# Reciprocal square root by logarithm and exponential, earlier input loads and a divided last product in an eight-core decoder step

## The chip, the cores and the metric

The kernel runs on all 8 cores of one Trainium2 chip (trn2). Each core does the same program on its own data. The time of a run is the device time of its slowest core, in microseconds (us). A program on eight cores has a slower state in some runs, in which the cores of one die (four of the eight) show a lower granted clock, that is the share of full speed that the profile records for TensorE; only runs outside that state ("fast") are compared, and where a median over all runs is given, the text says so. "The mean core" below is the mean over the eight cores of one fast profiled run.

## The reference

One step of a one-layer decoder: a mixer made of causal pooling and a gated short convolution, then a squared-ReLU MLP, with three RMS norms. Model width is 1024, MLP width 4096, eight prompts of 2048 tokens plus 16 meta tokens, and 512 sample tokens.

```python
def rmsnorm(x, g):
    y = x * lax.rsqrt(jnp.mean(x * x, axis=-1, keepdims=True) + EPS)
    return y * g

def layer(x, ...):
    hn = rmsnorm(x, norm1_g)
    proj = jnp.einsum('btd,de->bte', hn, w_in)      # u | B | C | h
    ...                                             # pooling mixer, y = B * conv3(C * h)
    x = x + jnp.einsum('bte,ed->btd', mix, w_out)
    hn = rmsnorm(x, norm2_g)
    a = jax.nn.relu(jnp.einsum('btd,df->btf', hn, w1))
    x = x + jnp.einsum('btf,fd->btd', a * a, w2)
    return x, ...
...
y_prompt = rmsnorm(xp, final_g)[:, N_META:]
```

## The kernel before

Each core holds one prompt and 64 sample tokens as 8 groups of 264 columns (features on partitions, tokens on columns); group 0 has 280 until the MLP, with the meta tokens. Groups 0 to 2 share the first reading of the input weights, in 16 blocks; groups 3 to 7 follow one by one through the mixer; then the MLP goes over four pairs of groups, twice, once for each half of its width. The MLP uses products of 2x2 blocks in seven multiplications. Early on the pooling weights are multiplied into the output weights (the "folding", eight matmuls of 512 columns). To copy a finished sum out of PSUM is called an eviction. A list scheduler orders each engine's queue from a table of costs written into the kernel, so a changed constant reorders everything.

All work goes through helpers, and the profile names those lines: L572 is a matmul, L594 a ScalarE activation, L597 a tensor_tensor on VectorE or GpSimd, L602 VectorE's scalar_tensor_tensor (two operations, two inputs, one scalar), L606 VectorE's reciprocal, and L618 a DMA (L615 after the change). "psall" is the PSUM, where the matmuls put their sums, "big" the SBUF, which holds everything else on the core. In the views PE is TensorE, PEld its weight loads, DVE VectorE, ACT ScalarE, POOL GpSimd and SPq the queue that issues most DMA transfers; "h2d" holds the normalised input of the MLP, "w1p" and "w2p" its weights.

The norm, used by all three RMS norms but for small differences:

```python
def rs_from(q, n):
    bank = alloc()
    r = ps(bank, n)
    for i in range(2):
        mm(r, ONEB[:], q[i], i == 0, i == 1)        # sum over partitions
    act(r, r, AF.Sqrt, scale=1.0 / D, bias=EPS)
    recip(r, r)
    return r, bank

def n1_ss(g):
    r, bank = rs_from(SQ_(g), NIN[g])
    for k in range(8):
        stt(HN[g][k], XT[g][k], cn(k), r, ALU.mult, ALU.mult)
    free(bank)
```

The convolution, in SBUF, and the order of the first loads and of the first 48 chunks (a chunk is eight matmuls: one weight block on one group):

```python
def conv(dst, z, m, st):
    act(dst, z[c, 2 * st:2 * st + m], AF.Copy, scale=cn(28 + 8 + c))
    stt(dst, z[c, st:st + m], cn(28 + 4 + c), dst, ALU.mult, ALU.add)
    stt(dst, z[c, 0:m], cn(28 + c), dst, ALU.mult, ALU.add)
# ...
for i in range(16):
    load_win(i, ...)                                # 0.5 MB each
ld["x1"] = load_x(1, [ld[0]], "sp")                 # group 1 after weight block 0
ld["x2"] = load_x(2, [ld[3]], "sp")                 # group 2 after weight block 3
# ...
todo = sorted((max(hn_t[g], w_t(i)), i, g) for i in range(16) for g in range(3))
for t, i, g in todo:
    if g not in seen:                               # first chunk of a group
        seen.add(g)
        if g > 0:
            n1_sq(g)                                # squares
            n1_ss(g)                                # sums, norm, products
    ...                                             # the chunk
```

At the end of the last pair the squares of all four quarters of a block are taken at once, two reciprocals follow, and sixteen scalings of 264 columns:

```python
def final(p):
    for h in range(2):
        ...
        mm(r, ONEF[:], FS[h], True, True, f32=True)
        act(r, r, AF.Sqrt, scale=1.0 / D, bias=EPS)
        recip(FS[h], r)
    for d in range(4):
        for q in range(4):
            stt(X[d][q], X[d][q], cn(16 + d + 4 * (q % 2)), FS[q // 2], ALU.mult, ALU.mult)
        finals.append(dma("sync", dr(yT[p, d]), X[d][:], 128 * 4 * GN * 4, tag="y"))
```

Of the kernel before, what the change touches and what calls it, by code (L numbers as in the profile page):

```python
# [84 lines left out]
class Prog:  # L85
# [87 lines left out]
    def schedule(self):  # L173
# [14 lines left out]
        for op in reversed(ops):  # L188
            full = op.dur + (2.0 + op.bytes / 300e3 if op.dma else 0.0)
            p = 0.0  # L190
            for s in succ[op.id]:
                lat = 0.06 if ops[s].eng == op.eng and not op.dma else LAT[op.eng]
                p = max(p, ops[s].prio + lat)
            p += full
            for s in follow[op.id]:
                p = max(p, ops[s].prio + op.dur)
            op.prio = p
# [17 lines left out]
        def release(i, t, op):  # L215
            nonlocal cnt
            for s in succ[i]:
                lat = 0.06 if ops[s].eng == op.eng and not op.dma else LAT[op.eng]
# [168 lines left out]
def build_nc():  # L387
# [211 lines left out]
    def stt(out, a, s, b, op0, op1):  # L599
# [3 lines left out]
                     [out], ins, cost("vector", out.n, "f"))  # L603

    def recip(out, a):
        return P.add("vector", lambda e: e.reciprocal(out=out.ap, in_=a.ap), [out], [a], cost("vector", out.n, "f"))  # L606
# [10 lines left out]
    def dma_(q, out, in_, nbytes, extra, tag, prev):  # L617
        return P.add(q, lambda e: e.dma_start(out=out.ap, in_=in_.ap), [out], [in_], 0.07 if q == "sync" else 0.95, dma=True,  # L618
# [24 lines left out]
    def load_x(g, extra=(), link=None):  # L643
        return dma("sync", XT[g][:], dr(xg[g - 1]), xb, extra=extra, tag="x%d" % g, link=link)

    ld["x0a"] = dma("sync", XT[0][0:4], dr(x0[:, 0:4]), 128 * 4 * 280 * 4, tag="x0a", link="sp")
    dma("sync", CN[0:40], dr(cst), 20480, tag="cst", link="sp")
# [7 lines left out]
    for i in range(16):  # L655
        load_win(i, {0: ["x0a"]}.get(i) and [ld["x0a"]] or [])
    ld["x1"] = load_x(1, [ld[0]], "sp")
    ld["x2"] = load_x(2, [ld[3]], "sp")
    dma("sync", PWR[:], dr(pwT), 1 << 18, extra=[ld[9]], tag="pw", link="sp")
    dma("gpsimd", WR[:], dr(wout[:, 0:4]), 2 * MB, tag="wr")  # L660
    dma("gpsimd", WOUT[4:6], dr(wout[:, 4:6]), MB, tag="wo")
    ld["wo"] = dma("gpsimd", WOUT[6:8], dr(wout[:, 6:8]), MB, tag="wo")
    ld["x3"] = load_x(3, [ld[15]], "sp")
    ld["x4"] = load_x(4, [ld["wo"]], "sp")

    def load_w1(b, c, extra=()):
        op = dma("gpsimd", W1[c][0:4], dr(w1p[b * 8 + c]), MB, extra=extra, tag="w1_%d_%d" % (b, c))
        tsums(W1[c])
        return op

    def load_w2(b, d):
        op = dma("gpsimd", W2[d][0:4], dr(w2p[b * 4 + d]), 2 * MB, tag="w2_%d_%d" % (b, d))
        tsums(W2[d])
        return op

    def tsums(W):
# [6 lines left out]
    def n1_sq(g, parts=2):  # L683
        for i in range(parts):
            s = slice(i * 8 // parts, (i + 1) * 8 // parts)
            act(SQ_(g)[s], XT[g][s], AF.Square)
        q = SQ_(g)
        tt("vector", q[0:4], q[0:4], q[4:8], ALU.add, "b")
        tt("vector", q[0:2], q[0:2], q[2:4], ALU.add, "b")
# [6 lines left out]
    def rs_from(q, n):  # L696
        bank = alloc()
        r = ps(bank, n)
        for i in range(2):
            mm(r, ONEB[:], q[i], i == 0, i == 1)  # L700
        act(r, r, AF.Sqrt, scale=1.0 / D, bias=EPS)
        recip(r, r)
        return r, bank

    def n1_ss(g):
        r, bank = rs_from(SQ_(g), NIN[g])
# [63 lines left out]
    def h_chunk(g, c):  # L770
# [15 lines left out]
        def conv(dst, z, m, st):  # L786
            act(dst, z[c, 2 * st:2 * st + m], AF.Copy, scale=cn(28 + 8 + c))
            stt(dst, z[c, st:st + m], cn(28 + 4 + c), dst, ALU.mult, ALU.add)
            stt(dst, z[c, 0:m], cn(28 + c), dst, ALU.mult, ALU.add)
# [32 lines left out]
    def n2_ss(g):  # L822
# [6 lines left out]
        if g % 2 == 1:  # L829
# [6 lines left out]
            dma("sync", dr(h2d[p], ("h2d", p)), H2P[0:7], 128 * 7 * 4 * GN * 2, tag="h2s")  # L836
# [4 lines left out]
    def fold():  # L841
# [3 lines left out]
        for c in range(4):  # L845
            for h in range(2):
# [3 lines left out]
                act(WOUT[c, h * 512:h * 512 + 512], r, AF.Copy)  # L850
# [21 lines left out]
    n1_sq(0, 4)  # L872
    n1_ss(0)
    hn_t = (9.6, 17.0, 23.0)
    w_t = lambda i: 8.2 + 1.65 * i + (3.2 if i > 1 else 0) + (3.2 if i > 4 else 0)
# [24 lines left out]
    for c in range(5):  # L900
        load_w1(0, c, [ld["x4"]])
# [13 lines left out]
    for g in range(4, 8):  # L915
# [14 lines left out]
        if g == 6:  # L930
            load_h2(0, 0)
# [8 lines left out]
    load_w2(0, 0)  # L940
# [12 lines left out]
    class Unit:  # L953
        def __init__(self, p, b):
            self.p = p
            self.b = b
            self.M = self.K = self.B = None

        def terms(self, j, dst, start, stop, ks):
            r = ps(dst, GN)  # L960
# [44 lines left out]
        m = property(lambda s: ps(s.M, GN))  # L1005
        k_ = property(lambda s: ps(s.K, GN))
        b_ = property(lambda s: ps(s.B, GN))
# [52 lines left out]
    class U2(Unit):  # L1060
        nk = 8

        def __init__(self, p, b, d):
            Unit.__init__(self, p, b)
            self.d = d
            self.X = X[d]
# [4 lines left out]
        def rhs(self, j, k):  # L1071
            return A2[k][AO[j]]
# [7 lines left out]
        def after2(self):  # L1080
            act(self.X[0], self.k_, AF.Copy)

        def after7(self):
            tt("vector", self.X[3], self.m, self.X[3], ALU.add)
            tt("vector", self.X[3], self.b_, self.X[3], ALU.add)

        def after4(self):
            tt("vector", self.X[2], self.m, self.X[2], ALU.add)

        def after3(self):  # L1090
            tt("vector", self.X[1], self.b_, self.X[1], ALU.add)
            if self.b == 0:
                dma("sync", dr(x1d[self.p, self.d], *[("x1d", self.p, self.d, j) for j in range(4)]), self.X[:], 128 * 4 * GN * 4, tag="xs")
            else:
                act(SQF[:], self.X[:], AF.Square)
                if self.d == 0:
                    tt("vector", FS[:], SQF[0:4:2], SQF[1:4:2], ALU.add)
                else:
                    tt("vector", SQF[0:4:2], SQF[0:4:2], SQF[1:4:2], ALU.add)
                    tt("vector", FS[:], FS[:], SQF[0:4:2], ALU.add)  # L1100

    def final(p):
# [126 lines left out]
```

## Time and profile before

| | before |
|---|---|
| median of the first 4 runs, one of them slow | 719.41 us (718.25 to 790.04) |
| spans of the eight cores in the profiled run | 709.8 to 716.7 us |
| mean granted TensorE clock | 0.952 to 0.957 |
| busy on the slowest core: TensorE, VectorE, ScalarE, GpSimd | 87%, 74%, 39%, 14% |

TensorE is the engine with the most work, but no engine is full. The useful question is where TensorE loses time, stage by stage, and what it waits for there; the prediction below does that. One line that it does not show is the chain of work that ended last, by engine, as shares of the span:

```profile
PE 58%; DVE 29%; DMA 6%; ACT 4%; issue 2%; POOL 0%; SPq 0%; DVEq 0%
```

### The profile page before, as it was taken

To read this page: it belongs to the slowest core of one execution; us is meant where nothing else is said; L and a number is where in the kernel's file an instruction comes from. 1 tells how busy PE (TensorE), PEld (TensorE's weight loads), DVE (VectorE), ACT (ScalarE), POOL (GpSimd) and SP (SyncE) were. 2 spreads that over 40 slices of the span, in tenths; PEclk is the share of its full clock that TensorE was granted. 3 is DMA by queue.
4 is the path that set the end of the run, shared out by engine and by line. 5 is a ranking of instruction groups with operands and counts; after the bars stand their busy time and mean duration, and the time that the engine had idled before them with its cause. 6 is when DMAs were issued, how large, how long until landed. Compare 5 with 4: busy or idle time off the path is not lost.

```text
span 716.7 us, 12912 instructions; the slowest of 8 cores (709.8 to 716.7 us)
## 1 busy us (share of the span) xinstructions
PE 623.1 (87%) x5175; PEld 512.8 (72%) x5176; DVE 528.4 (74%) x1302; ACT 282.9 (39%) x715; POOL 103.2 (14%) x121
## 2 busy tenths in 40 slices
PE   2469998598898958999999999989998998998991
PEld 0248886385665847788888888878887887787770
DVE  3556799869999778955746646968859859858866
ACT  2234632252332325505516417307347237337421
POOL 5554141043250800000000001110000000000000
PEclk9779999999998989999999999999999999999995
DMA  7993195832334797795153249999802801500602
GB/s 151 220 207 97 31 174 139 243 122 70 128 87 141 156 162 130 229 319 183 36 193 122 98 142 196 195 184 193 269 1 70 246 36 57 187 1 31 212 1 121
DMA packets 30395, 100.00 MB, mean 140 GB/s; under 512 B 4608, under 2 KB 13824, under 8 KB 26752
## 3 DMA queue, kind: packets, MB, share of 16 engines
q1 hardware_dynamic: 24144, 76.12, 32.7%
q0 software_dynamic: 6192, 23.07, 20.9%
q8 instruction: 40, 0.66, 0.4%
q14 instruction: 19, 0.16, 0.1%
HBM read 88.13 MB, written 34.11 MB: 171 GB/s over the span
## 4 chain that ended last, share of the span: by engine, by line
PE 58%; DVE 29%; DMA 6%; ACT 4%; issue 2%; POOL 0%; SPq 0%; DVEq 0%
PE psall L572 58%; DVE big L597 12%; DVE big L602 12%; DMA big<-w1p 4%; ACT big L594 3%; DVE psall L606 3%; DVE big L606 2%; DMA h2d<-big 2%; DMA big<-x 1%; DVE psall L597 0%; ACT psall L594 0%; SPq L618 0%; POOL big L618 0%; DVEq L327 0%; POOL big L756 0%
## 5 line engine op out<-in xcount | busy, mean ns | idle before, releaser
L572 PE MATMUL psall<-big 128*128 128x264 bf16 (+1 forms) x5175 | 623.1, 282 | 81.1 <-DVE big L597 35.2
L572 PEld LDWEIGHTS psall<-big 128*128 128x128 bf16 x5176 | 512.8, 100 | 190.6 <-DVE big L602 49.9
L597 DVE TENSOR_TENSOR big<-psall,big 128x264 f32<-128x264 f32 (+3 forms) x420 | 173.7, 425 | 120.7 <-PE psall L572 90.0
L594 ACT ACTIVATE big<-psall 128x264 f32<-128x264 f32 (+2 forms) x396 | 144.6, 389 | 223.9 <-PE psall L572 217.9
L597 DVE TENSOR_TENSOR big<-big 128x264 bf16<-128x264 bf16 (+6 forms) x428 | 167.6, 434 | 49.2 <-ACT big L594 40.8
L594 ACT ACTIVATE big<-big 128x264 bf16<-128x264 f32 (+6 forms) x230 | 125.0, 554 | 150.5 <-DVE big L597 143.0
L602 DVE SCALAR_TENSOR_TENSOR big<-big 128x264 bf16<-128x264 f32 (+3 forms) x264 | 116.9, 477 | 3.5 <-ACT big L594 2.0
L597 POOL TENSOR_TENSOR big<-big 128x528 bf16<-128x528 f32 (+14 forms) x54 | 72.0, 1345 | 44.3 <-ACT big L594 42.8
L602 DVE SCALAR_TENSOR_TENSOR big<-big,psall 128x264 bf16<-128x264 f32 (+1 forms) x128 | 52.6, 483 | 1.7 <-DMA h2d<-big 1.5
L594 ACT ACTIVATE psall<-psall 128x264 f32<-128x264 f32 (+1 forms) x88 | 32.9, 382 | 46.2 <-PE psall L572 33.3
L618 POOL DMA_DIRECT2D big<-w1p x16 | 8.6, 545 | 218.1 <-PE psall L572 196.7
L606 DVE RECIPROCAL psall<-psall 128x264 f32<-128x264 f32 (+1 forms) x16 | 28.9, 1813 | 3.0 <-ACT psall L594 3.0
L597 DVE TENSOR_TENSOR psall<-psall,big 128x264 f32<-128x264 f32 x32 | 13.9, 437 | 4.4 <-PE psall L572 2.7
L606 DVE RECIPROCAL big<-psall 128x264 f32<-128x264 f32 x8 | 14.0, 1780 | 1.7 <-ACT psall L594 1.7
L756 POOL COPY big<-big 128x2 f32<-128x2 f32 (+1 forms) x13 | 6.0, 462 | 60.8 <-DVE big L597 58.7
L618 POOL DMA_DIRECT2D big<-w2p x8 | 4.3, 540 | 51.7 <-PE psall L572 51.6
L618 POOL DMA_DIRECT2D big<-win x16 | 8.6, 594 | 5.3 <-DMA big<-x 5.3
L752 POOL COPY big<-big 128x64 f32<-128x64 f32 x7 | 2.8, 401 | 0.0
L618 POOL DMA_DIRECT2D big<-wout x3 | 1.8, 589 | 0.0
L594 ACT ACT_TABLE_LOAD x1 | 1.3, 1283 | 1.1 <-PEq L388 1.1
L622 DVE MEMSET big<- 128x128 bf16 (+1 forms) x2 | 0.3, 165 | 1.2 <-PEq L388 1.2
L843 DVE TENSOR_SCALAR big<-big 128x128 bf16<-128x128 f32 x4 | 0.9, 273 | 0.0
(4 smaller groups left out, 0.4 us busy)
## 6 DMA issues: line engine op xcount, KB each, us to landing
x1d<-big SPq DMA_DIRECT2D x32, 528.0 KB, 5.0
big<-x1d SPq DMA_DIRECT2D x32, 528.0 KB, 5.0
big<-h2d SPq DMA_DIRECT2D x8, 1848.0 KB, 11.3
yT<-big SPq DMA_DIRECT2D x16, 528.0 KB, 3.0
big<-w1p POOLq DMA_DIRECT2D x16, 512.0 KB, 10.2
big<-w2p POOLq DMA_DIRECT2D x8, 1024.0 KB, 14.9
big<-xg SPq DMA_DIRECT2D x7, 1056.0 KB, 9.0
h2d<-big SPq DMA_DIRECT2D x4, 1848.0 KB, 10.3
```

The source lines that it names most:

```text
L572: return P.add("tensor", lambda e: e.matmul(out=out.ap, lhsT=lhsT.ap, rhs=rhs.ap, start=start, stop=stop, skip_group_check=skip), [out], [ ...
L594: return P.add("scalar", lambda e: e.activation(out=out.ap, in_=in_.ap, func=func, **kw), [out], ins, d)
L597: return P.add(eng, lambda e: e.tensor_tensor(out=out.ap, in0=a.ap, in1=b.ap, op=op), [out], [a, b], cost(eng, out.n, kind))
L602: return P.add("vector", lambda e: e.scalar_tensor_tensor(out=out.ap, in0=a.ap, scalar=sv, in1=b.ap, op0=op0, op1=op1), [out], ins, cost(" ...
L606: return P.add("vector", lambda e: e.reciprocal(out=out.ap, in_=a.ap), [out], [a], cost("vector", out.n, "f"))
L618: return P.add(q, lambda e: e.dma_start(out=out.ap, in_=in_.ap), [out], [in_], 0.07 if q == "sync" else 0.95, dma=True, nbytes=nbytes, ext ...
L622: return P.add(eng, lambda e: e.memset(out.ap, v), [out], [], 0.1)
L752: P.add("gpsimd", lambda e: e.tensor_copy(out=U[g][:, 0:16].ap, in_=U[g - 1][:, 264:280].ap), [U[g][:, 0:16]], [U[g - 1][:, 264:280]], 0.2)
L756: P.add("gpsimd", lambda e: e.tensor_copy(out=Z[g][c, 0:2].ap, in_=Z[g - 1][c, 264:266].ap), [Z[g][c, 0:2]], [Z[g - 1][c, 264:266]], 0.1)
L843: P.add("vector", lambda e, c=c: e.tensor_scalar(out=PWS[c].ap, in0=PWR[c].ap, scalar1=cn(24 + c).ap, scalar2=1.0 / POOL_WIN[c], op0=ALU.m ...
```

## The change

The intent is to take VectorE and the loads out of TensorE's way in every stage at once:

1. The reciprocal square root is ln, then exp(-0.5 ln), both on ScalarE, in place of a square root on ScalarE and a reciprocal on VectorE.
2. Groups 1 and 2 are loaded right behind weight block 0; groups 1 to 4 are loaded from GpSimd's queue and the first MLP weights no longer wait for group 4. The squares of groups 0 to 2 come in quarters, and eight matmuls sum them in place of VectorE additions.
3. The convolution builds its sum in a PSUM bank; half of the folding evictions go to VectorE.
4. The last pair's second MLP product is cut into 168 and 96 columns, so that only 96 columns' norm and scaling remain after the last matmul, shared by GpSimd. In every pair the final norm's squares are now taken quarter by quarter, as each comes.
5. Scheduling constants, and two loads held until a store has landed.

```diff
-    def recip(out, a): ...
 # (cut; the next line is the scheduler's cost of a scalar_tensor_tensor)
+                     ..., cost("vector", out.n, "f") + (0.057 if isinstance(s, V) else 0.0))
 # (cut)
+    load_win(0, [ld["cst"]])
+    load_x(1)
+    load_x(2)
+    for i in range(1, 16):
+        load_win(i)
 # (cut)
-    def rs_from(q, n):
+    def rs_from(q, n, nq=2):
 # (cut)
-        act(r, r, AF.Sqrt, scale=1.0 / D, bias=EPS)
-        recip(r, r)
+        act(r, r, AF.Ln, scale=1.0 / D, bias=EPS)
+        act(r, r, AF.Exp, scale=-0.5)
 # (cut)
-        r, bank = rs_from(SQ_(g), NIN[g])
+        r, bank = rs_from(SQ_(g), NIN[g], 8 if g < 3 else 2)
 # (cut)
-            act(dst, z[c, 2 * st:2 * st + m], AF.Copy, scale=cn(28 + 8 + c))
-            stt(dst, z[c, st:st + m], cn(28 + 4 + c), dst, ALU.mult, ALU.add)
-            stt(dst, z[c, 0:m], cn(28 + c), dst, ALU.mult, ALU.add)
+            pb = alloc()
+            t = ps(pb, m)
+            act(t, z[c, 2 * st:2 * st + m], AF.Copy, scale=cn(28 + 8 + c))
+            stt(t, z[c, st:st + m], cn(28 + 4 + c), t, ALU.mult, ALU.add)
+            stt(dst, z[c, 0:m], cn(28 + c), t, ALU.mult, ALU.add)
+            free(pb)
 # (cut)
-    hn_t = (9.6, 17.0, 23.0)
-    w_t = lambda i: 8.2 + 1.65 * i + (3.2 if i > 1 else 0) + (3.2 if i > 4 else 0)
+    hn_t = (11.0, 16.5, 20.0)
+    w_t = lambda i: 10.5 + 1.7 * i + (7.0 if i else 0)
 # (cut)
-            load_h2(0, 0)
+            load_h2(0, 0, [ld["h2s", 2]])
 # (cut)
-    load_w2(0, 0)
+    load_w2(0, 0, [ld["h2s", 2]])
 # (cut)
+            last = b == 1 and p == NP - 1
+            for lo, n in (((0, GN - TN), (GN - TN, TN)) if last else ((0, GN),)):   # TN = 96
+                for t in range(2):
+                    groups.append([U2(p, b, 2 * t, lo, n, lo > 0), U2(p, b, 2 * t + 1, lo, n, lo > 0)])
 # (cut)
-    final(NP - 1)
+    final(NP - 1, GN - TN, TN, True)
```

## The prediction

> **What bounds the kernel now.** I read the list of cores first: spans 709.8 to 716.7 us, clocks 0.952 to 0.957, so no die is disturbed and core 2 can stand for all. TensorE is busy 87% of the span, so I asked not for the busy share but for what TensorE loses in each stage. I cut the span at the first matmul after the first three token groups' input projection (88), at the start of the unbroken MLP (306.5) and at the last MLP matmul (697.2). The view of stretches gives:
>
> ```profile
> core 2: us, PE busy (x) PEld busy (x) DVE busy (x) ACT busy (x) POOL busy (x), PEclk, DMA share, GB/s
> 0.00:88.00 88.00, 58.36 (x394) 40.81 (x396) 49.83 (x92) 33.72 (x71) 38.83 (x54) 0.88 0.70 144
> 88.00:306.50 218.50, 183.49 (x1448) 145.46 (x1445) 191.48 (x423) 81.44 (x197) 57.98 (x55) 0.93 0.60 148
> 306.50:697.20 390.70, 379.11 (x3332) 325.36 (x3332) 273.83 (x767) 165.20 (x445) 6.35 (x12) 1.00 0.48 135
> 697.20:716.70 19.50, 2.15 (x5) 1.18 (x4) 13.26 (x23) 2.54 (x4) 0.00 (x0) 0.61 0.27 111
> ```
>
> In the stretch from 323 to 403 TensorE never pauses: 713 matmuls in 80.0 us, 112.2 ns each. At that rate the first stage is worth 394 x 0.1122 = 44.2 us and loses 43.8; the second is worth 162.5 and loses 56.0; the MLP is worth 373.9 and loses 16.8; the end of 19.5 us is all loss. So 136 us of 717 can be attacked, and the change touches every stage.
>
> The timeline shows what the first stage loses: TensorE ends group 0's chunks at 22.8 and gets nothing to do until group 1 is normalised.
>
> ```profile
> 22.77 0.69 ACT L594 ACTIVATE big<-psall 128x280 f32<-128x280 f32 x2 [0.72 <-PE psall L572]
> ...
> 23.34 2.06 ACT L594 ACTIVATE big<-big 128x1056 bf16<-128x1056 f32 x2
> ...
> 25.43 4.54 DVE L597 TENSOR_TENSOR big<-big 128x1056 bf16<-128x1056 bf16 x2 [8.30 <-ACT big L594]
> ...
> 31.09 1.82 DVE L606 RECIPROCAL psall<-psall 128x264 f32<-128x264 f32 x1 [1.12 <-ACT psall L594]
> 32.94 3.29 DVE L602 SCALAR_TENSOR_TENSOR big<-big,psall 128x264 bf16<-128x264 f32 x8
> ...
> 33.48 10.89 PE L572 MATMUL psall<-big 128*128 128x264 bf16 x64 [2.84 <-DVE big L602]
> ```
>
> The squares of group 1 run at 23.3, behind group 0's evictions, two additions on VectorE take 4.5 us, the reciprocal 1.8, and the product with the norm feeds TensorE one matmul per 0.4 us. Group 2 repeats it (matmuls from 50.6).
>
> In the second stage VectorE is busy 191 of 218 us. Three rows of groups, the first from the page, the others from the view of groups by form in the first 306.5 us (count, busy us, mean ns of one, idle before):
>
> ```profile
> L606 DVE RECIPROCAL psall<-psall 128x264 f32<-128x264 f32 (+1 forms) x16 | 28.9, 1813 | 3.0 <-ACT psall L594 3.0
> ...
> L602 DVE SCALAR_TENSOR_TENSOR big<-big,psall 128x264 bf16<-128x264 f32 x120 | 49.2, 482 | 1.6 <-DMA h2d<-big 1.5
> ...
> L602 DVE SCALAR_TENSOR_TENSOR big<-big 128x264 f32<-128x264 f32 x56 | 31.8, 582 | 2.4 <-ACT big L594 2.0
> ```
>
> A reciprocal costs as much as four other VectorE operations of its size, and the convolution's products, both inputs in SBUF, cost 100 ns more than those with one input in PSUM. The end, from the timeline:
>
> ```profile
> 696.82 1.08 ACT L594 ACTIVATE big<-big 128x1056 f32<-128x1056 f32 x1 [4.58 <-DVE big L597]
> ...
> 703.74 1.81 DVE L606 RECIPROCAL big<-psall 128x264 f32<-128x264 f32 x1 [1.75 <-ACT psall L594]
> ...
> 707.71 6.05 DVE L602 SCALAR_TENSOR_TENSOR big<-big 128x264 f32<-128x264 f32 x15
> 708.94 5.18 SPq L618 DMA_DIRECT2D yT<-big  x4
> ```
>
> Nothing overlaps here: squares and sums until 702, two reciprocals, sixteen scalings until 713.8, then the last store.
>
> **What the Trainium skill says.** "ScalarE: Activation LUTs", section "Table sets: the hidden batching unit", puts exponential and logarithm into one set, with the cheap functions in every set. Then the new pair needs one table load. The trace has one load of 1.28 us for today's functions; it can't show the new set. "SBUF — State Buffer", section "SBUF: two separate sides", says that VectorE operations with two SBUF inputs and GpSimd lock each other out of a shared port pair. The trace agrees: the convolution's 200-column products took up to 1.57 us beside GpSimd and 0.37 without it, by single records. "TensorE: Matmul & The Clock Gate", section "Back-to-back issue gap", gives about 81 ns per matmul with weight load at 128 columns, more than its 56 of pure streaming. No matmul here is that narrow; a weight load lasts 99 ns in the groups' row and hides behind 112. Its Part 1 says that an idle TensorE falls to half clock and recovers after some 3.4 us: the granted share is 0.71 and 0.78 in the stretches 18 to 36 and 36 to 54.
>
> **The change, part by part.**
>
> *Start.* Groups 1 and 2 are loaded right after the first weight block, the squares are cut in four and summed by eight matmuls in place of two large additions, and the norm is two ScalarE passes. By 58.8 us the old kernel had read 17.2 MB (inputs, input and output weights, three groups), landing times from the trace: 303 GB/s, an estimate that I reuse. Constants, group 0 and block 0 are 1.7 MB, group 1 another 1.1: it lands near 12, group 2 near 15 to 16, then one 0.5 MB block per 1.7 us, block 15 near 41. Norm of group 1: four squares of 0.66, a few matmuls, two passes of 0.38, then 3.3 us of products: ready from about 17 to 20; group 2 to 24. TensorE needs 24 x 0.1122 = 2.7 us per block, more than the 1.7 of its arrival, so from about 22 it is its own bound: 48 chunks less the 4 or 5 done, 43 x 0.9 = 39, some half clock, the eight folding matmuls: 394 matmuls done near 67 where 88 stood. Saved 21.
>
> *Second stage.* 13 reciprocals of 1.81 lie in it and 9 of them stand in the chain (its view in order of time has them at 89, 102, 117, 159, 164, 196, 219, 224 and 282); each gives way to one pass of 0.38 plus a handover of about 0.1: 9 x 1.33 = 12 us. The 56 convolution products go from 582 to some 480 ns, 5.7 us of VectorE time, and the 8 short ones some 2; I take half of that as standing in TensorE's way (the view of waits gives it 32 us of waiting in this stage, nearly all on VectorE), so 3 to 4 and I count 2. Folding evictions shared by VectorE: nothing. Against it each convolution takes a PSUM bank for about two microseconds. Saved 14, before that.
>
> *MLP.* At each of three passages to a new token pair in the second half TensorE waits 1.9, 0.85 and 0.4 us while VectorE does reciprocals and scalings (waits put down to the reciprocal: 5.4 us). Without them two thirds go: 6 saved. Cutting the last pair's second product into 168 and 96 columns turns 224 matmuls into 448. By streaming alone this costs nothing; with 81 ns for each of both widths 224 x (162 - 112.2) = 11.2 us; with a full weight load of 98 each, 18.8. I take 5, nearer the streaming side, since the weight loads start as soon as the matmul before has started. Net saved 1.
>
> *End.* Only 96 columns remain: last addition, square, a matmul of sums, two passes and a copy, about 0.25 each with handovers 2 us; ten products on VectorE of 0.25 beside six on GpSimd, 2.6; the store 2.9 as now (713.8 to 716.7). That is 7.5 to 8 in place of 19.5. Saved 11.5.
>
> Sum 21 + 14 + 1 + 11.5 = 47.5, or 672. I take 4 back for PSUM banks and for the reordering of all engines' queues that the new cost constants bring: 676.
>
> **The rivals.** *The narrow matmuls are bound by their weight loads.* For: 99 ns per load, and the skill's 81. Against: the loads' spacing is never tested here. It makes the end of the MLP 6 to 14 us longer: 682 to 690. *The early gain is given back.* The second stage has its own chain: the store of the first residual activations runs from 125.1 to 138.5 and the next norm waits for it, and w1 blocks share the DMA. If that stage is bound by such transfers, removing reciprocals gains 4 and not 14, and part of the 21 waits for weights: 690 to 695. *Two function sets.* If the logarithm and the exponential, or either and the others, alternate between tables, 24 norms pay twice 1.28 us, and more with the drain; about 10 of them stand on the path: 25 us and more lost, 700 or above. The skill speaks against it. *Better than the sum:* TensorE's half-clock stretches in the second stage (0.93 on average, up to 15 us by that alone) close as well: 660.
>
> **Range and chances.** The middle is 676; the first rival alone or half the second gives 685 to 690, the last 660. Both rivals together give 695. So 658 to 695. For less than 2% gain (705) both rivals and more must come true, or the tables: 6%.
>
> **What would show it.** Right: 394 matmuls done by about 67 us; no reciprocals, one table load; convolution products with a PSUM input near 480 ns; no wait over 1 us at passages between pairs; under 9 us from last MLP matmul to the end. Wrong: the spacing of the 96-column matmuls near 100 ns; more than one table load; waits of TensorE on convolutions' banks; the first MLP product not earlier by 25 us than before.

## The result, and the profile after

The kernel after took 675.25 us (median of 11 runs, 674.3 to 722.39, slow ones included); the kernel before took 719.44 us over its 16 runs in those rounds. The ratio of after to before is 0.938, with a 95% interval of 0.9356 to 0.9405: faster by 6.2%. Every ratio here is the mean time of one kernel's fast runs over that of the other's of the same rounds, so not quite the ratio of the medians quoted. The output is correct.

The view of stretches of the slowest core after (core 7), cut at the marks of the prediction. Its columns are those shown there: start:end, length, then busy time and count of TensorE, its weight loads, VectorE, ScalarE and GpSimd, then the granted clock, the DMA share and GB/s. Eighteen matmuls of sums were added in the start, so 394 old matmuls are 412 here:

```profile
0.00:75.20 75.20, 59.49 (x413) 41.91 (x414) 38.14 (x85) 33.23 (x73) 39.71 (x59) 0.98 0.82 168
75.20:279.90 204.70, 172.84 (x1450) 141.73 (x1448) 172.37 (x410) 84.17 (x209) 57.54 (x55) 0.97 0.64 157
279.90:664.70 384.80, 381.28 (x3560) 330.64 (x3558) 274.32 (x847) 184.75 (x528) 6.33 (x12) 1.00 0.47 139
664.70:673.90 9.20, 1.81 (x17) 1.50 (x14) 5.18 (x23) 1.65 (x7) 2.10 (x6) 0.70 0.63 177
```

| stage, slowest core | before | after | saved | predicted |
|---|---|---|---|---|
| start | 88.0 | 75.2 | 12.8 | 21 |
| second stage | 218.5 | 204.7 | 13.8 | 14 |
| MLP | 390.7 | 384.8 | 5.9 | 1 |
| end | 19.5 | 9.2 | 10.3 | 11.5 |
| taken back | | | | -4 |
| sum | 716.7 | 673.9 | 42.8 | 43.5 |

So the total is right, the start was promised 8 too much and the MLP 5 too little. The granted clock of the first two stages rose from 0.88 and 0.93 to 0.98 and 0.97. In the first 27 us this record does not follow the matmuls: it says 1.00 from 24 to 27 us, where those of 264 columns start 0.22 us apart until 26.6 and 0.11 apart after that. And the chain that ended last has changed its make-up:

```profile
PE 59%; DVE 20%; DMA 15%; ACT 3%; issue 1%; POOL 0%; SPq 0%; DVEq 0%
```

VectorE lost nine points of the span, DMA gained nine: transfers now stand where VectorE stood.

**The start.** The timeline view (start, length, engine, line, operation, count, and in brackets how long the engine had been idle and for whom) answers to the lines of before at 22.8 to 33.5:

```profile
19.51 7.94 PE L572 MATMUL psall<-big 128*128 128x264 bf16 x32 [1.40 <-DVE big L602]
...
27.48 0.78 ACT L594 ACTIVATE psall<-psall 128x264 f32<-128x264 f32 x2 [0.44 <-PE psall L572]
28.30 3.29 DVE L602 SCALAR_TENSOR_TENSOR big<-big,psall 128x264 bf16<-128x264 f32 x8 [6.05 <-ACT psall L594]
28.84 20.48 PE L572 MATMUL psall<-big 128*128 128x264 bf16 x152 [1.40 <-DVE big L602]
```

The squares of group 2, four of 0.56 us from 18.84 on in the same view, end at 21.1. Its two norm passes, 0.39 us each, start only at 27.5, when TensorE has done 32 more matmuls in 7.94 us (0.25 us each, twice the full-speed spacing): 24 of chunks, and then the eight sums. VectorE idled 6.05 us for it. After 28.8 TensorE runs without a break for 20 us.

**The second stage.** The view of TensorE's waits gives who was waited for, total, count and the longest. Before (88 to 306.5 us):

```profile
PE psall L572 <- DVE big L602: 19.8, 10, 7.5
```

After (75.2 to 279.9 us):

```profile
PE psall L572 <- DMA big<-h2d: 8.8, 1, 8.8
PE psall L572 <- DVE big L602: 8.7, 4, 3.3
```

The wait for VectorE's products with the norm fell from 19.8 to 8.7 us, its longest, of 7.5 us, is gone, and a DMA wait of 8.8 us has come in: the load of the normalised activations of the first pair ("h2d"), in front of the MLP. Two lines of the timeline show the load's issue and the matmul that it held up:

```profile
217.78 0.33 SPq L615 DMA_DIRECT2D big<-h2d  x1
...
234.06 2.36 PE L572 MATMUL psall<-big 128*128 128x264 bf16 x10 [8.75 <-DMA big<-h2d]
```

**The end.** From the timeline after the last MLP matmul at 664.7, answering to the lines of before at 696.8 to 708.9:

```profile
666.02 0.50 ACT L594 ACTIVATE psall<-psall 128x96 f32<-128x96 f32 x2 [0.22 <-PE psall L572]
667.56 2.10 POOL L597 TENSOR_TENSOR big<-big 128x96 f32<-128x96 f32 x6 [211.75 <-DVE big L1146]
667.56 2.33 DVE L602 SCALAR_TENSOR_TENSOR big<-big,psall 128x96 f32<-128x96 f32 x10
```

Norm and scalings are done at 669.9; before they ended 16.6 us behind the last matmul (713.8 less 697.2), here 5.2.

### The profile page after: what moved, and what is told of

The parts are those of the page before. It is cut to its first block, busy times and chain, and to the rows that moved or that the text cites. A ratio compares the mean times of both kernels' runs of the same rounds, so it can differ in the third digit from the quotient of the medians.

```text
span 673.9 us, 13606 instructions; the slowest of 8 cores (665.7 to 673.9 us)
## 1 busy us (share of the span) xinstructions
PE 615.4 (91%) x5430; PEld 515.8 (77%) x5430; DVE 490.0 (73%) x1361; ACT 303.8 (45%) x816; POOL 105.7 (16%) x132
## 4 chain that ended last, share of the span: by engine, by line
PE 59%; DVE 20%; DMA 15%; ACT 3%; issue 1%; POOL 0%; SPq 0%; DVEq 0%
PE psall L572 59%; DVE big L597 11%; DVE big L602 7%; DMA h2d<-big 4%; DMA big<-w2p 4%; DMA big<-w1p 3%; DMA big<-h2d 2%; ACT big L594 2%; DMA big<-x 1%; ACT psall L594 1%; DMA big<-x1d 1%; DVE psall L602 1%; DVE big L849 0%; DVE psall L597 0%; POOL big L597 0%
## 5 line engine op out<-in xcount | busy, mean ns | idle before, releaser
L572 PE MATMUL psall<-big 128*128 128x264 bf16 (+4 forms) x5430 | 615.4, 275 | 51.2 <-DVE big L602 14.8
L572 PEld LDWEIGHTS psall<-big 128*128 128x128 bf16 (+1 forms) x5430 | 515.8, 99 | 150.7 <-DVE big L602 29.8
L597 DVE TENSOR_TENSOR big<-psall,big 128x264 f32<-128x264 f32 (+5 forms) x440 | 175.2, 411 | 113.0 <-PE psall L572 68.3
L594 ACT ACTIVATE big<-psall 128x264 f32<-128x264 f32 (+3 forms) x404 | 147.1, 384 | 210.6 <-PE psall L572 202.6
L597 DVE TENSOR_TENSOR big<-big 128x264 bf16<-128x264 bf16 (+8 forms) x461 | 173.0, 412 | 41.6 <-ACT big L594 21.6
L597 POOL TENSOR_TENSOR big<-big 128x528 bf16<-128x528 f32 (+15 forms) x60 | 75.4, 1271 | 253.8 <-DVE big L1146 211.7
L602 DVE SCALAR_TENSOR_TENSOR big<-big,psall 128x264 bf16<-128x264 f32 (+4 forms) x174 | 70.7, 466 | 12.9 <-ACT psall L594 12.5
L602 DVE SCALAR_TENSOR_TENSOR big<-big 128x264 bf16<-128x264 f32 (+2 forms) x192 | 76.8, 436 | 1.1
L594 ACT ACTIVATE psall<-psall 128x264 f32<-128x264 f32 (+3 forms) x108 | 39.1, 374 | 27.6 <-PE psall L572 25.5
L594 ACT ACTIVATE psall<-big 128x264 f32<-128x264 f32 (+2 forms) x36 | 16.2, 458 | 29.6 <-DVE big L597 29.3
L602 DVE SCALAR_TENSOR_TENSOR psall<-big,psall 128x264 f32<-128x264 f32 (+2 forms) x36 | 16.3, 459 | 1.3 <-ACT psall L594 1.3
L849 DVE TENSOR_SCALAR big<-big 128x128 bf16<-128x128 f32 x4 | 4.2, 1061 | 0.0
## 6 DMA issues: line engine op xcount, KB each, us to landing
big<-xg POOLq DMA_DIRECT2D x4, 1056.0 KB, 27.5
```

Source lines behind the costliest of these rows:

```text
L572: return P.add("tensor", lambda e: e.matmul(out=out.ap, lhsT=lhsT.ap, rhs=rhs.ap, start=start, stop=stop, skip_group_check=skip), [out], [ ...
L594: return P.add("scalar", lambda e: e.activation(out=out.ap, in_=in_.ap, func=func, **kw), [out], ins, d)
L597: return P.add(eng, lambda e: e.tensor_tensor(out=out.ap, in0=a.ap, in1=b.ap, op=op), [out], [a, b], cost(eng, out.n, kind))
L602: return P.add("vector", lambda e: e.scalar_tensor_tensor(out=out.ap, in0=a.ap, scalar=sv, in1=b.ap, op0=op0, op1=op1), [out], ins, cost(" ...
L849: P.add("vector", lambda e, c=c: e.tensor_scalar(out=PWS[c].ap, in0=PWR[c].ap, scalar1=cn(24 + c).ap, scalar2=1.0 / POOL_WIN[c], op0=ALU.m ...
```

## The experiments

The theory was that each part acts where the prediction put it: the norm pair in all stages, the early loads in the start, the PSUM convolution a little, the split at the end. The rivals: that the narrow matmuls pay for their weight loads, that a transfer takes the place of a removed wait, and that new constants in the scheduler, not the parts themselves, move the time.

To compare stages over kernels with different matmul counts, I used marks on every core and took the mean core: the start lasts to the first 512-column folding matmul, the second stage to the same MLP matmul counted back from the last (3331 before it; 3559 with the split, which adds 224 matmuls and puts four fp32 sums in front of the last), the MLP to the last matmul's start. They lie a few microseconds from the prediction's marks.

| mean core, us | start | second | MLP | end | span | slowest core |
|---|---|---|---|---|---|---|
| before | 83.1 | 222.0 | 389.7 | 19.8 | 714.7 | 716.7 |
| after | 70.5 | 205.9 | 383.8 | 9.3 | 669.5 | 673.9 |
| e1, norm pair alone | 80.3 | 207.8 | 381.5 | 16.7 | 686.3 | 689.7 |
| e3, old loads | 75.5 | 206.1 | 383.6 | 9.3 | 674.5 | 679.5 |
| e8, group 2's sums first | 65.2 | 206.7 | 383.9 | 9.3 | 665.2 | 669.5 |
| e5, convolution in SBUF | 73.2 | 211.3 | 383.7 | 9.3 | 677.5 | 683.6 |
| c, old constants | 68.9 | 209.6 | 383.8 | 9.0 | 671.2 | 677.3 |
| e2, no split | 70.8 | 205.4 | 380.3 | 13.5 | 670.0 | 674.9 |
| e16, e8 and shared scalings | 65.1 | 206.5 | 385.5 | 9.0 | 666.0 | 669.3 |
| e4, free load | 70.6 | 204.9 | 381.8 | 9.3 | 666.6 | 673.9 |
| e10, load in seven parts | 70.6 | 209.1 | 382.5 | 9.3 | 671.5 | 676.5 |
| e12, weights behind the load | 70.3 | 206.6 | 383.8 | 9.3 | 670.0 | 674.3 |
| e14, e8 and e12 | 65.1 | 207.1 | 384.4 | 9.3 | 665.9 | 670.0 |
| e15, e14 with the load free | 65.1 | 208.0 | 381.7 | 9.3 | 664.1 | 670.2 |

The table is of one profiled run each, and small differences in it say little: over its eleven fast runs the mean core of the kernel after has a span of 667.2 to 669.8 us (668.5 on the mean), the profiled one being near the top.

All twelve gave correct results. Edits are against the kernel after, unless said.

### e1: the norm pair alone, in the kernel before

```diff
-        act(r, r, AF.Sqrt, scale=1.0 / D, bias=EPS)
-        recip(r, r)
+        act(r, r, AF.Ln, scale=1.0 / D, bias=EPS)
+        act(r, r, AF.Exp, scale=-0.5)
 # and in final():
-            act(r, r, AF.Sqrt, scale=1.0 / D, bias=EPS)
-            recip(FS[h], r)
+            act(r, r, AF.Ln, scale=1.0 / D, bias=EPS)
+            act(FS[h], r, AF.Exp, scale=-0.5)
```

> The kernel before, with only the reciprocal replaced by the logarithm and exponential pair. If the reciprocals on VectorE held the chain as the prediction counted (12 us in the second stage, about 4 in the start, 5 at the passages between pairs, 3 at the end), the time falls by 20 to 26 us, to about 696. If the chain only named them and other VectorE work or the DMA stores take their place, the gain is under 10 us.

Measured: fast runs 689.23 to 691.23 us, ratio 0.9579 (0.955 to 0.9609). The mean core saves 28.4 us: 2.9 in the start, 14.2 in the second stage, 8.2 in the MLP, 3.1 at the end. The groups of its trace hold one table load, of 1.28 us, as before.

So this one part is about two thirds of the whole gain of 44 us, the two functions share a table, and the rival of two table sets is dead. Of the wait in front of the MLP something more is to be seen in the timeline:

```profile
243.98 3.29 DVE L602 SCALAR_TENSOR_TENSOR big<-big,psall 128x264 bf16<-128x264 f32 x8 [2.09 <-DMA h2d<-big]
...
247.32 5.02 PE L572 MATMUL psall<-big 128*128 128x264 bf16 x22 [8.03 <-DVE big L602]
```

TensorE waits 8.03 us for VectorE, but VectorE itself had waited for a store of activations ("h2d<-big") before it could overwrite its buffer: issued at 225.3, the store landed at 243.95. The name in the view of waits is the last link only; behind it stands the transfer, here already.

### e3: the old order of loads

```diff
-    load_win(0, [ld["cst"]])
-    load_x(1)
-    load_x(2)
-    for i in range(1, 16):
-        load_win(i)
+    for i in range(16):
+        load_win(i, {0: ["x0a"]}.get(i) and [ld["x0a"]] or [])
+    ld["x1"] = load_x(1, [ld[0]], "sp")
+    ld["x2"] = load_x(2, [ld[3]], "sp")
 # (cut: the other loads, hn_t and w_t as before)
```

> The changed kernel with the old order of loads and the old order constants of the first stage; sums by matmuls and the new norm stay. If the early arrival of groups 1 and 2 is what the first stage gained, its 394 old matmuls end near 86 us in place of 75 and the time rises by 9 to 12 us. If the gain came from the sums on TensorE and the shorter norm, the time rises by less than 4.

Measured: 681.12 us, ratio 0.9448 (0.9419 to 0.9478). The start is 5.0 us longer on the mean core, the other stages agree within 0.2. The early loads, with the order constants that belong to them, are worth 5.0 us, between the 9 to 12 and the "less than 4" that were expected; nothing of it is given back later: that rival is wrong for these loads.

### e8: the sums of group 2 ahead of the next weight block

The timeline after suggested that group 2's eight matmuls of sums stand in TensorE's queue behind the chunks of the next weight blocks. The edit asks for squares and sums of group 2 before weight block 1:

```diff
     for t, i, g in todo:
         e = EO[i]
+        if i == 1 and 2 not in seen:
+            seen.add(2)
+            n1_sq(2)
+            n1_ss(2)
```

> The changed kernel with group 2's squares and sums put ahead of the chunks of the second weight block in TensorE's order. In the changed kernel group 2's products start at 28.3 us though its squares are done at 21.1. If that order is the failed part of my start estimate, they start near 25 and the first stage ends 2 to 3 us earlier. Rival: the clock's half rate and block arrivals bound it, and the stage ends within 1 us of 70.5 (mean of the cores).

Measured: 670.2 us (668.72 to 670.99, four fast runs); no run of the kernel after was below 674.3. The ratio to before is 0.9283 (0.9206 to 0.9359, wide since the runs of before were disturbed). The timeline:

```profile
19.51 12.66 PE L572 MATMUL psall<-big 128*128 128x264 bf16 x68 [1.40 <-DVE big L602]
...
24.51 0.79 ACT L594 ACTIVATE psall<-psall 128x264 f32<-128x264 f32 x2 [1.09 <-PE psall L572]
25.33 3.29 DVE L602 SCALAR_TENSOR_TENSOR big<-big,psall 128x264 bf16<-128x264 f32 x8 [3.08 <-ACT psall L594]
```

The products of group 2 start at 25.33 and not at 28.30, and the start is 5.3 us shorter (65.2 against 70.5). That is more than the 2 to 3 expected, and more than the 3.0 by which group 2 starts earlier: in the kernel after TensorE also waits for VectorE for 2.0 us at 51.2, and in this trace it never waits between 19.51 and the end of the stage. So some 3.0 us are the place of eight small matmuls in an in-order queue, and some 2.0 a later wait that went with it, which the expectation did not count. This is the best version: it beats both kernels, by 5 us the one after.

### e5: the convolution in SBUF again

```diff
-            pb = alloc()
-            t = ps(pb, m)
-            act(t, z[c, 2 * st:2 * st + m], AF.Copy, scale=cn(28 + 8 + c))
-            stt(t, z[c, st:st + m], cn(28 + 4 + c), t, ALU.mult, ALU.add)
-            stt(dst, z[c, 0:m], cn(28 + c), t, ALU.mult, ALU.add)
-            free(pb)
+            act(dst, z[c, 2 * st:2 * st + m], AF.Copy, scale=cn(28 + 8 + c))
+            stt(dst, z[c, st:st + m], cn(28 + 4 + c), dst, ALU.mult, ALU.add)
+            stt(dst, z[c, 0:m], cn(28 + c), dst, ALU.mult, ALU.add)
```

> The changed kernel with the convolution's partial results in SBUF again, as before. By the prediction PSUM is worth 2 to 4 us in the second stage (56 products at 582 instead of 480 ns): the time rises by 2 to 4 us and the products with two SBUF inputs come back over 550 ns. Rival: the shorter products hide, or the freed PSUM banks pay them back, and the time stays within 1.5 us.

Measured: 681.98 us, ratio 0.9463 (0.9396 to 0.9531). The mean core loses 8.0 us: 5.4 in the second stage, 2.7 in the start. The view of groups by form (count, busy us, mean ns of one, idle before), first the kernel after:

```profile
L602 DVE SCALAR_TENSOR_TENSOR psall<-big,psall 128x264 f32<-128x264 f32 x28 | 13.7, 489 | 1.3 <-ACT psall L594 1.3
L602 DVE SCALAR_TENSOR_TENSOR big<-big,psall 128x264 f32<-128x264 f32 x28 | 13.4, 483 | 0.4
```

and this experiment:

```profile
L602 DVE SCALAR_TENSOR_TENSOR big<-big 128x264 f32<-128x264 f32 x56 | 37.3, 681 | 3.5 <-ACT big L594 3.1
```

With two SBUF inputs the product takes 681 ns, more than the 582 of the kernel before; with one in PSUM 486. The 56 products cost 37.3 us and 27.1 (13.7 + 13.4), and the time rises by 7 us where 2 to 4 were expected. These means mix two kinds, which the single records part by whether an operation of GpSimd runs at the same time. Alone, 34 of the 56 products take 488 ns, no more than with one input in PSUM; beside GpSimd 22 take 979, up to 2271. With one input in PSUM they take 482 to 490 either way. That agrees with the lock between VectorE and GpSimd that the Trainium skill states ("SBUF — State Buffer", section "SBUF: two separate sides"). In the kernel before 38 lay alone (479 ns) and 18 beside GpSimd (800): in this order more of them meet GpSimd, and each is held longer.

### c_consts: the old scheduling constants

```diff
-                lat = 0.09 if ops[s].eng == op.eng and not op.dma else LAT[op.eng]
+                lat = 0.06 if ops[s].eng == op.eng and not op.dma else LAT[op.eng]
 # (twice)
-                     ..., cost("vector", out.n, "f") + (0.057 if isinstance(s, V) else 0.0))
+                     ..., cost("vector", out.n, "f"))
-        ... 0.07 if q == "sync" else 0.7, ...
+        ... 0.07 if q == "sync" else 0.95, ...
```

> The changed kernel with the scheduler's cost constants as before (0.06 for a handover on one engine, no 0.057 for a per-partition scalar, 0.95 for an issue). The constants change only the order of the engines' queues. I counted them as noise of about 4 us together with PSUM banks: the time should stay within 4 us of 675. If the order is worth more than the parts, it rises by over 4.

Measured: 677.93 us, ratio 0.9397 (0.9334 to 0.946), against 0.938 of the kernel after. The start is 1.6 us shorter and the second stage 3.7 longer. The intervals overlap; by the medians, and by the mean core over all fast runs (671.6 against 668.5), the constants are worth about three microseconds, and do not make the gain.

### e2: no division of the last product

```diff
-            last = b == 1 and p == NP - 1
+            last = False
 # (cut: the end's order of products as in the other groups)
-    final(NP - 1, GN - TN, TN, True)
+    final(NP - 1)
```

> The changed kernel without the cut of the last pair into 168 and 96 columns. By my theory the cut costs under 1 us of TensorE (its matmuls run at 72 and 42 ns in the changed kernel's trace) and takes 4 to 6 us off the end, so this kernel is 4 to 6 us slower than the changed one, near 680. If the narrow matmuls had a hidden cost (11 us by the estimate of 81 ns each), this kernel would be faster than the changed one.

Measured: fast runs 676.44 to 678.38 us, ratio 0.9403 (0.9374 to 0.9432). Undivided, the end is 13.5 us and not 9.3, but the MLP 380.3 and not 383.8. So of the 4.2 us that the split takes off the end it puts 3.5 on the MLP. The whole spans differ by 0.5 us in the two profiled runs (670.0 and 669.5 on the mean core) and by 2.7 over all fast runs (671.2 and 668.5); the medians of the fast runs are 678.05 and 675.25. The intervals of the ratios overlap: the split is worth some 0.5 to 3 us, not the 4 to 6 that were expected. In the kernel after, two stretches of 6.0 and 2.8 us show the divided products at work, the first at 168 and the second at 96 columns:

```profile
643.00:649.00 6.00, 6.00 (x86) 6.00 (x84) 4.90 (x19) 2.07 (x7) 0.00 (x0) 1.00 0.01 3
659.20:662.00 2.80, 2.80 (x71) 2.80 (x68) 2.80 (x16) 2.44 (x10) 0.00 (x0) 1.00 0.03 9
```

The counts include a few matmuls that were still in flight when the stretch began. Read from record to record over all 221 pairs of each width, the median distance from start to start is 73 ns at 168 columns and 43 at 96, against 113 at 264. The weight loads of the same time:

```profile
L572 PEld LDWEIGHTS psall<-big 128*128 128x128 bf16 x73 | 3.2, 98 | 0.0
```

Each load's record lasts 98 ns, but 73 of them lie in a stretch of 3 us: they overlap each other. So 73 + 43 = 116 against 113 ns, times 224, is 0.7 us for the whole division. The first rival, a floor of 81 ns or of a full load, is wrong. From the first 168-column matmul to the start of the last one of 96 columns core 7 needs 29.4 us; the same products undivided, with the 16 other matmuls that lie between, need 26.9 in e2. Of these 2.5 us, 0.7 are the streaming, 0.6 are four fp32 sums of the first part (142 to 212 ns each), which now lie inside the stretch, and 1.2 are four pauses, the longest of 0.55 us behind VectorE in the timeline. The other 1.0 or so lies earlier in the MLP and was not traced.

### e16: e8, and half of the first part's scalings on ScalarE and GpSimd

```diff
 # (on top of e8)
-                if not tail:
+                if not tail and n < GN and d >= 2:
+                    act(x, x, AF.Copy, scale=fg)
+                    tt("gpsimd", x, x, FS[q // 2, lo:hi], ALU.mult)
+                elif not tail:
                     stt(x, x, fg, FS[q // 2, lo:hi], ALU.mult, ALU.mult)
```

> Group 2's sums first, and half of the first part's final scalings (eight of sixteen, 168 columns) moved from VectorE to ScalarE and GpSimd. In the changed kernel six of these sixteen stand in VectorE's queue after the last MLP matmul (1.8 us), and VectorE is busy 7.8 of the 8.7 us before. If VectorE's queue is what the cut of the last pair costs, the end (9.3 us) falls to 7 to 8 and the time by 1 to 3 us below the 670 of the run with the sums first. Rival: ScalarE or GpSimd[...] ends later than VectorE did, and nothing is gained.

Measured: fast runs 670.08 to 673.11 us, ratio 0.9326 (0.9274 to 0.9379); no better than e8. The timeline of it shows why:

```profile
652.30 1.88 DVE L602 SCALAR_TENSOR_TENSOR big<-big 128x168 f32<-128x168 f32 x3
```

GpSimd has eight products of the same shape from 652.26 to 656.7. Three of VectorE's scalings take 1.88 us beside them; three of the same shape took 0.99 us in the kernel after, with GpSimd idle. By single records the four that lie beside GpSimd take 634 ns on the mean and the other four 382. VectorE has eight scalings fewer, but pays for the others. Both operands lie in SBUF, so it looks like e5's loss again. The pauses of the divided product remain.

### e4: the activations' load not held for the store

The wait of 8.8 us in front of the MLP could come from the new condition that the load of the first pair's activations waits for the store of the third pair's. The condition is an order of transfers only; without it the kernel is still correct.

```diff
-            load_h2(0, 0, [ld["h2s", 2]])
+            load_h2(0, 0)
```

> The changed kernel without the added rule that the first load of the MLP input waits for the third pair's store. My theory: this rule made a new wait, 8.8 us of TensorE at 234 us in the changed kernel; without it the load starts some 10 us earlier and the time falls by 5 to 8 us, to about 668. Rival: load and store share the same DMA engines, the wait moves to the store or to the next norm, and the time stays within 2 us of 675.

Measured: 676.11 us, ratio 0.9376 (0.9345 to 0.9408): the same as after. The mean core gains 2.9 us (1.5 over all fast runs), the slowest none: its span is 673.9 as before the edit. The second stage spreads over 198.9 to 211.8 us by core (after: 202.9 to 209.0). On the unlucky core 6 the chain in order of time has a store of activations of 15.3 us (from 207.8) and then this weight load:

```profile
228.29 20.68 DMA big<-w2p
```

It lands at 249, and a wait of TensorE of 8.3 us ends at 251. On core 2 the same two took 12.72 and 13.36 us, and no wait there was over 2.9 us. So the condition costs the early cores something and makes the cores more alike; on the late ones it is not the cause, since a wait as long stands there without it, now for weights.

### e10: the same load in seven parts

If only the first blocks of the load are needed by the first product, seven small loads should let TensorE begin earlier.

```diff
-            load_h2(0, 0, [ld["h2s", 2]])
+            for j in (0, 3, 4, 1, 5, 6, 2):
+                dma("sync", H2[0][j], dr(h2d[0, :, j], ("h2d", 0)), ..., extra=[ld["h2s", 2]], tag="h2l")
```

> The changed kernel with the first load of the MLP input cut into seven loads, one per factor, in the order of use; the rule that they wait for the third pair's store stays. The first product needs one factor in seven. If TensorE's wait of 7 to 10 us at about 230 us is for bytes that it does not need yet, it falls to under 2 us on every core and the time by 5 to 8 us, to about 668. Rival: later factors or the weights hold the next products up just as long, and the gain is under 2.

Measured: fast runs 678.03 to 687.05 us, ratio 0.9441 (0.9325 to 0.9558); not better. In the view of waits, two waits for the load (7.1 and 4.9 us) take the place of the one of 8.8. The timeline of the slowest core:

```profile
226.98 1.07 PE L572 MATMUL psall<-big 128*128 128x264 bf16 x8 [0.53 <-DVE big L602]
...
228.74 1.06 PE L572 MATMUL psall<-big 128*128 128x264 bf16 x8 [0.68 <-DVE big L597]
...
236.89 1.92 PE L572 MATMUL psall<-big 128*128 128x264 bf16 x8 [7.10 <-DMA big<-h2d]
...
243.67 6.53 PE L572 MATMUL psall<-big 128*128 128x264 bf16 x42 [4.86 <-DMA big<-h2d]
```

By the records the first two parts were issued at 220.7 and 221.1, landed at 226.2 and 228.6, and were used at once. The third, of 264 KB, was issued at 221.5 and landed at 236.8: 15.2 us, nearly as long as the whole load of 1848 KB in one piece in the kernel after (217.8 to 233.9, 16.1 us). So the size of the part that TensorE waits for does not set the wait. What the DMA engines have to do beside it may: in the kernel after their busy share is 1.0 from 208 to 232 us.

### e12: the weights of the second product behind the load

```diff
-            load_h2(0, 0, [ld["h2s", 2]])
+            ld["h2l"] = load_h2(0, 0, [ld["h2s", 2]])
-    load_w2(0, 0, [ld["h2s", 2]])
+    load_w2(0, 0, [ld["h2l"]])
```

> The changed kernel with the first two w2 loads waiting for the first load of the MLP input instead of for the third pair's store. In the changed kernel the w2 loads take 43 to 63% of the DMA engines' time between 224 and 232 us, while TensorE waits for the MLP input until 234. If sharing the DMA engines makes that wait, it falls from 7 to 10 us to 3 to 5 and the second stage by 4 to 5 us, the time to about 671. Rival: HBM or the other core of a pair bounds the load, and the gain is under 1.5 us, or the later w2 loads hold up the MLP by as much.

Measured: the median of all six runs is 686.69 us, but three of them were slow; the fast ones are 675.86, 677.79 and 677.89, ratio 0.9405 (0.9377 to 0.9433). The longest wait of the slowest core is 8.8 us, as in the kernel after. That these weights follow so closely does not cause it.

### e14 and e15: e8 joined with e12, and with the load free

```diff
 # e14: the edits of e8 and of e12
 # e15: as e14, but
+            ld["h2l"] = load_h2(0, 0)
```

> Group 2's sums first (5 us alone in its run) and the w2 loads after the MLP input together. If the two are independent the time is 675 less 5 less the gain of the w2 change, about 666; if the earlier start only makes the DMA waits longer, it stays at 670.

> As the combination, and the first load of the MLP input no longer waits for the third pair's store. Freed alone it helped some cores by 8 us and left the slowest where they were. If it was the w2 loads that kept those back, all cores gain now, and the time falls to 660 to 664; if the store and the load slow each other, the slowest core stays within 2 us of the combination's.

Measured: e14 fast runs 670.63 to 671.5 us, ratio 0.9319 (0.9296 to 0.9343); e15 670.87 us, ratio 0.9311 (0.9279 to 0.9342). Both repeat e8's start of 65.1 us, so that gain is confirmed three times (with e16), and neither adds to it. In e15 the mean core is 1.1 us better than in e8 and the slowest 0.7 worse, as in e4.

## Why the prediction was right, and where its steps were not

The total (676 against 675.25) was right. Four terms were mis-sized: the start by -8.2, the end by -1.2, the MLP by +4.9, and the 4 us taken back were not lost. That these cancel to less than one is luck. Of the five signs of being right three came; the 394 matmuls were done at 75.2 and not by 67, and the end took 9.2 and not under 9. One reading of the lines was wrong in its figures: the 200-column products took 1.84 and 1.04 us beside GpSimd and 0.35 to 0.43 without it by the records, not 1.57 and 0.37.

**The start: 21 predicted, 12.8 measured.** The step that failed is "so from about 22 it is its own bound". The prediction expected 4 or 5 chunks done by then; 4 were done (32 matmuls, besides 24 of sums) when, only at 28.8, TensorE came to be fed without a break: 6.8 us late. The prediction gave a norm's sums "a few matmuls" without asking where they stand in TensorE's queue: squares done at 21.1, norm passes at 27.5. e8 moves them and group 2 starts 3.0 earlier. A part was also that the two groups landed at 15.0 and 18.0 us, where "near 12" and "15 to 16" stood. A second piece: the four folding scalings on VectorE, by the groups' rows, take 1061 ns each after and took 273 before (three of the four lie beside GpSimd now, at 1324 ns on the mean, the one alone takes 273); TensorE waits 2.0 us at 51.2 behind them, a wait that is gone in e8. Of the 12.7 us on the mean core, e3 gives 5.0 to the loads, e1 2.9 to the norm pair and e5 2.7 to the convolution in PSUM, and c says that the new constants cost 1.6. The other 3.7 (quartered squares, sums on TensorE) were not measured by themselves; as the parts were added to one kernel or taken from another, they need not add up.

**The second stage: 14 predicted, 13.8 measured.** The sum fits, its parts less so. The norm pair by itself gave 14.2 where 12 were predicted. The convolution was given 2, and undoing it costs 5.4 here and 2.7 in the start; the step "I take half of that as standing in TensorE's way" was too low, and it compared with 582 ns where the alternative in the new order was 681, taking for a fixed cost of two SBUF inputs what only the products beside GpSimd pay. The parts do not add up to the whole (14.2 + 5.4 + 3.7 for the constants is more than 16.2 on the mean core), and I take it, without a run for it, that the wait in front of the MLP limits them together.

**That wait is the rival that half came true.** The prediction's second rival, "The early gain is given back", named this stage's transfers. The gain of the stage was kept, but the last wait stayed at about 8 us under a new name: before 7.5 us for VectorE, in e1 8.0 for VectorE which waited for a store, after 8.8 for the load. Five orders of these transfers (after, e4, e10 and e12, and e15 against e8) gave no better time. That points to the sum of bytes which must pass between 208 and 232 us, with the DMA engines full, and not to any one condition; as every experiment changed the order and none the bytes, this is argued and not shown.

**The MLP: 1 predicted, 5.9 measured.** "Two thirds go" was too low for the passages: on the mean core the norm pair saves 8.2, and of the nine pauses before (1.9, 0.85 and 0.4 us at each of three passages, 9.5 us) only one of 0.48 us at each is left. "I take 5" for the narrow matmuls was too much: 3.5 on the mean core; the divided product itself costs 2.5 on core 7, of which 0.7 are streaming. The first rival, the bound by weight loads, did not happen.

**The end: 11.5 predicted, 10.3 measured.** The parts on the mean core: 3.1 by the norm pair (e1), then 3.2 more by the rest of the change without the split, in which each quarter's square is taken as it comes (from 16.7 in e1 to 13.5 in e2), then 4.2 by the split. So two undramatic edits give 6.3 of the 10.5, and the split pays 3.5 of its 4.2 back in the MLP.

**The 4 us taken back for banks and reordering** were not there: the constants help by about 3 us. The four waits of the second stage behind VectorE's L602 each follow a run of five to ten products with the norm (bf16, in the timeline); none follows a convolution's product alone, so I saw no wait for a convolution's bank.

**Table sets:** one load, as predicted. **Better than the sum:** the clock did recover (0.954 to 0.981 on the mean of the cores), but this is inside the stage sums, and the total did not go below them.

**Left open:** why, in the kernel after and its variants, one core of each pair of neighbours (0 and 1, 2 and 3, and so on) is mostly later: 672.4 and 666.8, 670.7 and 665.7, 672.4 and 666.0, 673.9 and 667.8 us in the profiled run. As the slowest core sets the time, some 4 us lie between the mean core and the result. Which of the two it is changes from run to run. The transfers around 208 to 232 us differ between such cores (e4), but nothing was run that would tell the cause.

## What to carry to other kernels

Price an operation by where it stands in an in-order queue, not only by its length: eight sums worth 1 us stood 5 us behind their squares in the queue, and moving them let the group start 3 us earlier and cleared a later wait of 2. When the view of waits names an engine, ask what that engine waited for, since a wait of the same length may stand behind it under another name. And before giving GpSimd a share of VectorE's work in SBUF, put one operand in PSUM, or count on slower products on VectorE (here 979 ns in place of 488).

## What the Trainium skill lacked or had wrong

- "TensorE: Matmul & The Clock Gate", section "Back-to-back issue gap": it gives about 81 ns per matmul with its weight load at 128 columns. Here the distance was 73 ns at 168 columns and 43 ns at 96, each with its own weight load whose record lasts 98 ns. The page's formula for the single gap (columns / 2.4 plus 2.5 ns: 72.5 and 42.5) fits these, so the sustained figure is no floor.
- "SBUF — State Buffer", section "SBUF: two separate sides": it states the lock between VectorE and GpSimd, and that the other fully blocks, but gives no time for operations of such sizes. Here, with GpSimd idle and beside it, VectorE's 264-column products with both inputs in SBUF took 488 and 979 ns (with one in PSUM 482 to 490 either way), 168-column scalings 382 and 634 ns, and 128-column scalings of the weights, with one tensor as input, 273 and 1324 ns.
- "ScalarE: Activation LUTs": its section "What it computes" advises VectorE's reciprocal with a square root for the reciprocal square root. Here that reciprocal took 1.81 us for 264 columns, and ln then exp, two passes of 0.39 us in one table set, gave correct results and 28.4 us on the mean core. The page has no figure for the reciprocal, and I found none on a VectorE page.
- No page of those I read tells how far two neighbouring cores differ that run the same program: here 5.0 to 6.4 us in a span of 670, with the cause open.
